# Rotary embedding in fp32 on one core: one GpSimd product over eight positions, paired PSUM banks, and the last stores on the other queue

## The chip, the cores and the metric

The kernel runs on one core of a Trainium2 chip. The metric is the device time of one execution in microseconds (us); the median of several executions counts, and lower is better.

## What is computed

```python
def reference(x, cos, sin):           # x: (8, 2048, 8, 64), cos and sin: (2048, 32), all float32
    x1 = x[..., : x.shape[-1] // 2]
    x2 = x[..., x.shape[-1] // 2 :]
    cos = cos[None, :, None, :]
    sin = sin[None, :, None, :]
    out1 = x1 * cos - x2 * sin
    out2 = x1 * sin + x2 * cos
    return np.concatenate([out1, out2], axis=-1)
```

Every head of 64 values is two halves of 32. Each output element is one element times a cosine, plus the element of the other half times a sine, whose sign is negative in the first half. The tables depend on the position in the sequence alone, so all eight heads and all eight batches share them.

## The kernel before, in words

**Layout.** The 2048 positions of a batch lie on 128 partitions, 16 consecutive positions on each. A position holds 8 heads of 64 values, so 512 floats; a batch is 8192 floats per partition, 4 MB in all. The tables are 16 x 32 floats per partition. The work goes by units of four positions (2048 floats per partition); batch 0 begins and batch 7 ends with two units of two positions.

**Loads and stores.** `xpool` has five tiles of a whole batch. Loads (line 67) are issued by SyncE (SP in the profile), that of batch 0 in three pieces with the tables between them. The first five batches are loaded ahead; the load of batch b + 5 (line 189) uses the tile of batch b and so waits until the stores of batch b have landed. The result is written over the input in the same tile. Stores (line 74) are issued by ScalarE (ACT): three pieces for batch 0, one for each of batches 1 to 6, three for batch 7. The text calls S6 or "store 6" the store of batch 6.

**One unit** (`rotate`, line 101) is made in one of three ways.
- Kind A, most units: GpSimd (POOL) makes two sine products into a tile `t2` in SBUF (line 121): the second output half from the first input half by `sin_sb`, and the first from the second by `nsin`, the negated table. VectorE (DVE) makes the cosine product into `t1` in PSUM (line 128), and adds the two into the batch's tile (line 135).
- Kind B, the first unit of batches 2, 4 and 5: the same products, with `t1` in SBUF, but TensorE (PE) adds them. For each 512 floats, two matmuls by the identity `eye` go into one PSUM bank `o`, the first for `t1` and the second for `t2` (lines 140 and 141), and ScalarE copies the bank into the batch's tile (line 142).
- Kind C, the first unit of batches 1 and 3: VectorE makes both products (lines 128 and 145), and TensorE adds them with `eye` and its negative `neye` (lines 156 and 157), ScalarE copies (line 161). GpSimd does nothing.

**What sets the order.** `keep` fixes the order of the instructions of each engine as they are written: unit by unit, batch by batch. So a store waits in ScalarE's stream until its batch is done, ahead of the copies of the next batch; the add of a unit stands on VectorE ahead of the next unit's cosine product. Semaphores are placed by the framework. A tile of a pool is given out again once all that reads or writes it is done. `t2` has three buffers of one unit each, `t1` in PSUM one (four banks), `t1s` in SBUF two, `o` two banks. The tables `cos_ps` and `sin_ps` hold two banks more[...].

**The beginning.** GpSimd makes `eye`; ScalarE makes `nsin`, `sin_ps` and `neye` (lines 89 to 91); VectorE copies the cosines to PSUM (line 92).

Of the kernel before, what the change touches and what calls it, by code (L numbers as in the profile page):

```python
# [9 lines left out]
@with_exitstack  # L10
def kernel(
    ctx: ExitStack,
    tc: tile.TileContext,
    x: bass.AP,
    cos: bass.AP,
    sin: bass.AP,
    out: bass.AP,
):
    nc = tc.nc
    keep = tc.keep_in_program_order  # L20
    f32 = mybir.dt.float32
    PSUM = bass.MemoryType.PSUM

    B, S, H, D = x.shape
    Dh = D // 2
    P = 128
    HD = H * D
    R = S // P
    ROW = R * HD
    UNIT = 4 * HD  # L30
    NBUF = 5
    C = 512
    last = B - 1

    xv = x.rearrange("b (q r) h d -> b q (r h d)", q=P)
    ov = out.rearrange("b (q r) h d -> b q (r h d)", q=P)
    cos_src = cos.rearrange("(q r) d -> q r d", q=P)
    sin_src = sin.rearrange("(q r) d -> q r d", q=P)

    const_pool = ctx.enter_context(tc.tile_pool(name="const", bufs=1))  # L40
    tab_pool = ctx.enter_context(tc.tile_pool(name="tab", bufs=1, space=PSUM))
    t1_pool = ctx.enter_context(tc.tile_pool(name="t1p", bufs=1, space=PSUM))
    o_pool = ctx.enter_context(tc.tile_pool(name="op", bufs=2, space=PSUM))
    t1s_pool = ctx.enter_context(tc.tile_pool(name="t1s", bufs=2))
    xpool = ctx.enter_context(tc.tile_pool(name="xpool", bufs=NBUF))
    t2_pool = ctx.enter_context(tc.tile_pool(name="t2p", bufs=3))

    cos_sb = const_pool.tile([P, R, Dh], f32, tag="cb")
    sin_sb = const_pool.tile([P, R, Dh], f32, tag="sb")
    nsin = const_pool.tile([P, R, Dh], f32, tag="ns")  # L50
    eye = const_pool.tile([P, P], f32, tag="eye")
    neye = const_pool.tile([P, P], f32, tag="neye")
    cos_ps = tab_pool.tile([P, R, Dh], f32, tag="cp")
    sin_ps = tab_pool.tile([P, R, Dh], f32, tag="sp")

    xts = {}

    def spans(sizes):
        lo = 0
        for n in sizes:  # L60
            yield lo, n
            lo += n

    def load(b):
        xt = xpool.tile([P, ROW], f32, tag="xt", name=f"xt{b}")
        for lo, n in spans([UNIT, UNIT, 2 * UNIT] if b == 0 else [ROW]):
            keep(nc.sync.dma_start(out=xt[:, lo : lo + n], in_=xv[b, :, lo : lo + n]))  # L67
            if b == 0 and lo == 0:
                keep(nc.sync.dma_start(out=cos_sb, in_=cos_src))  # L69
                keep(nc.sync.dma_start(out=sin_sb, in_=sin_src))  # L70
        xts[b] = xt

    def store(b, lo, n):
        keep(nc.scalar.dma_start(out=ov[b, :, lo : lo + n], in_=xts[b][:, lo : lo + n]))  # L74

    for b in range(NBUF):
        load(b)

    nc.gpsimd.memset(eye, 0.0)  # L79
    nc.gpsimd.affine_select(  # L80
        out=eye,
        in_=eye,
        compare_op=mybir.AluOpType.not_equal,
        fill=1.0,
        base=0,
        pattern=[[-1, P]],
        channel_multiplier=1,
    )
    keep(nc.scalar.mul(nsin, sin_sb, -1.0))  # L89
    keep(nc.scalar.copy(sin_ps, sin_sb))  # L90
    keep(nc.scalar.mul(neye, eye, -1.0))
    keep(nc.vector.tensor_copy(cos_ps, cos_sb))  # L92

    def rep(a, n):
        return dataclasses.replace(a, ap=[a.ap[0][:], a.ap[1][:], [0, n], a.ap[-1][:]])

    kinds = {}
    for b, kind in ((1, "C"), (2, "B"), (3, "C"), (4, "B"), (5, "B")):
        kinds[(b, 0)] = kind

    def rotate(b, lo, n):
        kind = kinds.get((b, lo), "A")
        xt = xts[b][:, lo : lo + n]
        r0 = lo // HD
        nr = n // HD
        xk = xt.rearrange("p (r k d) -> p r k d", r=nr, d=Dh)
        xu = xt.rearrange("p (g u d) -> p g u d", u=2, d=Dh)
        if kind == "A":
            t1 = t1_pool.tile([P, n], f32, tag="t1")
        else:  # L110
            t1 = t1s_pool.tile([P, n], f32, tag="t1s")
        if kind == "C":
            t2 = t1s_pool.tile([P, n], f32, tag="t1s")
        else:
            t2 = t2_pool.tile([P, n], f32, tag="t2")
        t1u = t1.rearrange("p (g u d) -> p g u d", u=2, d=Dh)
        t2u = t2.rearrange("p (g u d) -> p g u d", u=2, d=Dh)
        if kind != "C":
            for u, tab in ((1, sin_sb), (0, nsin)):
                keep(  # L120
                    nc.gpsimd.tensor_mul(  # L121
                        out=t2u[:, :, u, :].rearrange("p (r h) d -> p r h d", h=H),
                        in0=xu[:, :, 1 - u, :].rearrange("p (r h) d -> p r h d", h=H),
                        in1=rep(tab[:, r0 : r0 + nr, :], H),
                    )
                )
        keep(
            nc.vector.tensor_mul(  # L128
                out=t1.rearrange("p (r k d) -> p r k d", r=nr, d=Dh),
                in0=xk,  # L130
                in1=rep(cos_ps[:, r0 : r0 + nr, :], 2 * H),
            )
        )
        if kind == "A":
            keep(nc.vector.tensor_add(out=xt, in0=t1, in1=t2))  # L135
        elif kind == "B":
            for j in range(n // C):
                o = o_pool.tile([P, C], f32, tag="o")
                cs = slice(j * C, (j + 1) * C)
                nc.tensor.matmul(o, eye, t1[:, cs], start=True, stop=False)  # L140
                nc.tensor.matmul(o, eye, t2[:, cs], start=False, stop=True)  # L141
                keep(nc.scalar.copy(xt[:, cs], o))  # L142
        else:
            keep(
                nc.vector.tensor_mul(  # L145
                    out=t2.rearrange("p (r k d) -> p r k d", r=nr, d=Dh),
                    in0=xk,
                    in1=rep(sin_ps[:, r0 : r0 + nr, :], 2 * H),
                )
            )  # L150
            G = C // Dh
            for u in range(2):
                for j in range(n // 2 // C):
                    o = o_pool.tile([P, C], f32, tag="o")
                    gs = slice(j * G, (j + 1) * G)
                    nc.tensor.matmul(o, eye, t1u[:, gs, u, :], start=True, stop=False)  # L156
                    nc.tensor.matmul(  # L157
                        o, eye if u else neye, t2u[:, gs, 1 - u, :], start=False, stop=True
                    )
                    keep(  # L160
                        nc.scalar.copy(  # L161
                            xu[:, gs, u, :], o.rearrange("p (g d) -> p g d", d=Dh)
                        )
                    )

    def pieces(b):
        if b == 0:
            return [2 * HD, 2 * HD, UNIT, UNIT, UNIT]
        if b == last:
            return [UNIT, UNIT, UNIT, 2 * HD, 2 * HD]  # L170
        return [UNIT] * 4

    def shares(b):
        if b == 0:
            return [HD, 7 * HD, 2 * UNIT]
        if b == last:
            return [2 * UNIT, UNIT, UNIT]
        return [ROW]

    for b in range(B):  # L180
        done = 0
        outs = list(spans(shares(b)))
        for lo, n in spans(pieces(b)):
            rotate(b, lo, n)
            done = lo + n
            while outs and sum(outs[0]) <= done:
                store(b, *outs.pop(0))
        if b + NBUF <= last:
            load(b + NBUF)
# [30 lines left out]
```

## Time and profile before

| what | value |
|---|---|
| median of 8 executions | 163.46 us (163.33 to 164.02) |
| the profiled execution | 163.58 us |
| its span, first to last instruction | 161.7 us |
| VectorE busy | 140.1 us (87%), 66 instructions |
| GpSimd busy | 139.0 us (86%), 70 instructions |
| TensorE busy (matmuls) | 46.8 us (29%) |
| ScalarE busy | 14.3 us (9%) |
| moved by DMA | 67.65 MB, 418 GB/s over the span |

In the profile's slices the span is cut into 40 equal parts, and a digit is the busy share of a part in tenths, 9 meaning 90% or more. A queue line gives packets, MB, and the time that its packets took as a share of 16 DMA engines. A line of the chain of waits is start, duration, and what the time was spent on. A group line is line, engine and operation, output and inputs, shapes and count; then busy us and mean ns of one; then the idle time just before, and what ended most of it. A timeline line is start, duration, engine and line, with idle time before and its releaser in brackets. The fp32 matmuls stand in the trace as two records each (the "x2" of the timeline), 80 records for 40 matmuls.

### The profile page before, as it was taken

How to read it: one execution, taken by the hardware profiler on the slowest of the kernel's cores; microseconds unless marked ns; L12 is line 12 of the kernel's file. 1: busy time of each engine (PE TensorE's matmuls, PEld its weight loads, DVE VectorE, ACT ScalarE, POOL GpSimd, SP SyncE). 2: the span in 40 equal slices, each digit the busy share in tenths (PEclk: the TensorE clock that was granted, in tenths of full speed). 3: DMA queues.
4: the chain of work that ended last, by engine and by line, in shares of the span. 5: the costliest groups of instructions: out<-in, count | busy, mean ns of one | idle time of the engine just before them, and what ended most of it. 6: DMA issues, size and time to landing. Idle time of an engine off the chain costs nothing.

```text
span 161.7 us, 467 instructions
## 1 busy us (share of the span) xinstructions
PE 46.8 (29%) x80; PEld 18.6 (12%) x80; DVE 140.1 (87%) x66; ACT 14.3 (9%) x24; POOL 139.0 (86%) x70
## 2 busy tenths in 40 slices
PE   0000000399108940895029902990000000000000
PEld 0000000134003410331014301430000000000000
DVE  0458899999999999999999999999899998999900
ACT  3200000012100220022001310121000000000000
POOL 1299999999999899998996999998999979999200
PEclk9999999999855998579556995599655555555555
DMA  5999999899999999999999999999999999999994
GB/s 190 411 436 492 439 397 403 376 427 485 413 393 438 446 478 389 438 470 389 454 454 389 462 448 389 454 446 397 454 440 397 470 430 397 478 421 405 421 415 201
DMA packets 3458, 67.65 MB, mean 418 GB/s; under 512 B 384, under 2 KB 384, under 8 KB 768
## 3 DMA queue, kind: packets, MB, share of 16 engines
q1 hardware_dynamic: 1728, 34.08, 49.8%
q10 hardware_dynamic: 1728, 33.56, 48.2%
q14 instruction: 2, 0.02, 0.0%
HBM read 34.08 MB, written 33.55 MB: 418 GB/s over the span
## 4 chain that ended last, share of the span: by engine, by line
DMA 46%; DVE 37%; POOL 9%; issue 2%; SPq 1%; DVEq 0%; POOLq 0%; ACTq 0%
DMA xt<-in_x_dram 24%; DMA out_dram<-xt 19%; DVE t L128 18%; DVE xt L135 17%; POOL t L121 9%; DMA sin_sb<-in_sin_dram 3%; DVE t L145 1%; SPq L69 0%; SPq L67 0%; DVEq L135 0%; POOLq L121 0%; ACTq L74 0%
## 5 line engine op out<-in xcount | busy, mean ns | idle before, releaser
L121 POOL TENSOR_TENSOR t<-xt,sin_sb 128x1024 f32<-128x1024 f32 (+1 forms) x32 | 70.4, 2201 | 10.8 <-DMA sin_sb<-in_sin_dram 5.9
L128 DVE TENSOR_TENSOR t<-xt,cos_ps 128x2048 f32<-128x2048 f32 (+1 forms) x34 | 73.4, 2167 | 0.8
L121 POOL TENSOR_TENSOR t<-xt,nsin 128x1024 f32<-128x1024 f32 (+1 forms) x32 | 70.5, 2202 | 0.0
L135 DVE TENSOR_TENSOR xt<-t,t 128x2048 f32<-128x2048 f32 (+1 forms) x29 | 62.2, 2144 | 6.3 <-POOL t L121 3.8
L140 PE MATMUL o<-t,eye 128*128 128x512 f32 x24 | 16.0, 755 | 24.6 <-DVE t L128 24.6
L156 PE MATMUL o<-t,eye 128*128 128x512 f32 x16 | 11.7, 838 | 37.9 <-DVE t L128 37.9
L141 PE MATMUL o<-t,eye 128*128 128x512 f32 x24 | 14.9, 708 | 0.0
L142 ACT COPY xt<-o 128x512 f32<-128x512 f32 x12 | 7.0, 585 | 44.8 <-PE o L141 44.8
L140 PEld LDWEIGHTS o<-t,eye 128*128 128x128 f32 x24 | 5.7, 251 | 32.9 <-issue 32.9
L156 PEld LDWEIGHTS o<-t,eye 128*128 128x128 f32 x16 | 3.8, 257 | 42.8 <-POOL t L121 30.8
L161 ACT COPY xt<-o 128x512 f32<-128x512 f32 x8 | 4.7, 586 | 45.1 <-DVE t L128 26.6
L141 PEld LDWEIGHTS o<-t,eye 128*128 128x128 f32 x24 | 5.4, 227 | 7.8 <-issue 7.8
L92 DVE COPY cos_ps<-cos_sb 128x512 f32<-128x512 f32 x1 | 0.7, 695 | 6.2 <-DMA cos_sb<-in_cos_dram 6.2
L157 PE MATMUL o<-t,neye 128*128 128x512 f32 x8 | 5.6, 818 | 0.2 <-DVE t L145 0.2
L145 DVE TENSOR_TENSOR t<-xt,sin_ps 128x2048 f32<-128x2048 f32 x2 | 4.6, 2280 | 0.0
L157 PE MATMUL o<-t,eye 128*128 128x512 f32 x8 | 4.1, 592 | 0.0
L157 PEld LDWEIGHTS o<-t,neye 128*128 128x128 f32 x8 | 2.2, 294 | 4.5 <-issue 4.5
L157 PEld LDWEIGHTS o<-t,eye 128*128 128x128 f32 x8 | 1.5, 190 | 1.9 <-issue 1.9
L89 ACT ACT_TABLE_LOAD x1 | 1.3, 1283 | 0.7 <-PEq L204 0.7
L89 ACT ACTIVATE nsin<-sin_sb 128x512 f32<-128x512 f32 x1 | 0.6, 630 | 5.1 <-DMA sin_sb<-in_sin_dram 5.1
L90 ACT COPY sin_ps<-sin_sb 128x512 f32<-128x512 f32 x1 | 0.6, 579 | 0.0
L79 POOL MEMSET eye<- 128x128 f32 x1 | 0.2, 204 | 0.3 <-POOLq L204 0.3
(6 smaller groups left out, 1.0 us busy)
## 6 DMA issues: line engine op xcount, KB each, us to landing
xt<-in_x_dram SPq DMA_DIRECT2D x7, 4096.0 KB, 38.1
out_dram<-xt ACTq DMA_DIRECT2D x6, 4096.0 KB, 28.7
out_dram<-xt ACTq DMA_DIRECT2D x2, 2048.0 KB, 19.3
xt<-in_x_dram SPq DMA_DIRECT2D x2, 1024.0 KB, 6.1
xt<-in_x_dram SPq DMA_DIRECT2D x1, 2048.0 KB, 11.7
out_dram<-xt ACTq DMA_DIRECT2D x2, 1024.0 KB, 8.8
out_dram<-xt ACTq DMA_DIRECT2D x1, 1792.0 KB, 21.1
cos_sb<-in_cos_dram SPq DMA_DIRECT2D x1, 256.0 KB, 5.0
```

Source lines behind the costliest of these rows:

```text
L89: keep(nc.scalar.mul(nsin, sin_sb, -1.0))
L92: keep(nc.vector.tensor_copy(cos_ps, cos_sb))
L121: nc.gpsimd.tensor_mul(out=t2u[:, :, u, :].rearrange("p (r h) d -> p r h d", h=H), in0=xu[:, :, 1 - u, :].rearrange("p (r h) d -> p r h d" ...
L128: nc.vector.tensor_mul(out=t1.rearrange("p (r k d) -> p r k d", r=nr, d=Dh), in0=xk, in1=rep(cos_ps[:, r0 : r0 + nr, :], 2 * H),)
L135: keep(nc.vector.tensor_add(out=xt, in0=t1, in1=t2))
L140: nc.tensor.matmul(o, eye, t1[:, cs], start=True, stop=False)
L141: nc.tensor.matmul(o, eye, t2[:, cs], start=False, stop=True)
L142: keep(nc.scalar.copy(xt[:, cs], o))
L145: nc.vector.tensor_mul(out=t2.rearrange("p (r k d) -> p r k d", r=nr, d=Dh), in0=xk, in1=rep(sin_ps[:, r0 : r0 + nr, :], 2 * H),)
L156: nc.tensor.matmul(o, eye, t1u[:, gs, u, :], start=True, stop=False)
L157: nc.tensor.matmul(o, eye if u else neye, t2u[:, gs, 1 - u, :], start=False, stop=True)
L161: nc.scalar.copy(xu[:, gs, u, :], o.rearrange("p (g d) -> p g d", d=Dh))
```

## The change

Sync's queue issues the stores of the last batch. A unit of TensorE's sum is now four matmuls into two PSUM banks and one ScalarE copy of 1024 floats, with one such pair of banks. A sine product is one GpSimd instruction over eight positions (two of two and one of four at the beginning, two of four at the end): its input reads the two halves of each head in reversed order, by a negative step, and its table `sgn` holds minus sine and sine side by side, made by ScalarE in four passes. VectorE takes a product in parts of four positions. `t2` has two buffers of eight positions, `t1s` one, which first holds the tables as loaded. Kind C, `sin_ps` and `neye` are gone; the first unit of batches 1 to 5 is added on TensorE. The last batch's final positions go by units of four, not two of two.

```diff
--- before.py
+++ after.py
@@ -27,9 +27,9 @@
     HD = H * D
     R = S // P
     ROW = R * HD
-    UNIT = 4 * HD
     NBUF = 5
     C = 512
+    T = 4
     last = B - 1
 
     xv = x.rearrange("b (q r) h d -> b q (r h d)", q=P)
@@ -40,20 +40,22 @@
     const_pool = ctx.enter_context(tc.tile_pool(name="const", bufs=1))
     tab_pool = ctx.enter_context(tc.tile_pool(name="tab", bufs=1, space=PSUM))
     t1_pool = ctx.enter_context(tc.tile_pool(name="t1p", bufs=1, space=PSUM))
-    o_pool = ctx.enter_context(tc.tile_pool(name="op", bufs=2, space=PSUM))
-    t1s_pool = ctx.enter_context(tc.tile_pool(name="t1s", bufs=2))
+    o_pool = ctx.enter_context(tc.tile_pool(name="op", bufs=1, space=PSUM))
+    t1s_pool = ctx.enter_context(tc.tile_pool(name="t1s", bufs=1))
     xpool = ctx.enter_context(tc.tile_pool(name="xpool", bufs=NBUF))
-    t2_pool = ctx.enter_context(tc.tile_pool(name="t2p", bufs=3))
+    t2_pool = ctx.enter_context(tc.tile_pool(name="t2p", bufs=2))
 
-    cos_sb = const_pool.tile([P, R, Dh], f32, tag="cb")
-    sin_sb = const_pool.tile([P, R, Dh], f32, tag="sb")
-    nsin = const_pool.tile([P, R, Dh], f32, tag="ns")
+    tabs = t1s_pool.tile([P, 2, R, Dh], f32, tag="t1s", name="tabs")
+    cos_sb = tabs[:, 0, :, :]
+    sin_sb = tabs[:, 1, :, :]
+    sgn = const_pool.tile([P, R, 2, Dh], f32, tag="sg")
     eye = const_pool.tile([P, P], f32, tag="eye")
-    neye = const_pool.tile([P, P], f32, tag="neye")
     cos_ps = tab_pool.tile([P, R, Dh], f32, tag="cp")
-    sin_ps = tab_pool.tile([P, R, Dh], f32, tag="sp")
 
-    xts = {}
+    loads = {0: [4, 4, 8]}
+    products = {0: [2, 2, 4, 8], last: [8, 4, 4]}
+    stores = {0: [1, 7, 8], last: [8, 4, 4]}
+    on_tensor = {(b, 0) for b in range(1, 6)}
 
     def spans(sizes):
         lo = 0
@@ -61,17 +63,22 @@
             yield lo, n
             lo += n
 
+    xts = {}
+
     def load(b):
         xt = xpool.tile([P, ROW], f32, tag="xt", name=f"xt{b}")
-        for lo, n in spans([UNIT, UNIT, 2 * UNIT] if b == 0 else [ROW]):
-            keep(nc.sync.dma_start(out=xt[:, lo : lo + n], in_=xv[b, :, lo : lo + n]))
+        for lo, n in spans(loads.get(b, [R])):
+            cs = slice(lo * HD, (lo + n) * HD)
+            keep(nc.sync.dma_start(out=xt[:, cs], in_=xv[b, :, cs]))
             if b == 0 and lo == 0:
                 keep(nc.sync.dma_start(out=cos_sb, in_=cos_src))
                 keep(nc.sync.dma_start(out=sin_sb, in_=sin_src))
         xts[b] = xt
 
     def store(b, lo, n):
-        keep(nc.scalar.dma_start(out=ov[b, :, lo : lo + n], in_=xts[b][:, lo : lo + n]))
+        cs = slice(lo * HD, (lo + n) * HD)
+        queue = nc.sync if b == last else nc.scalar
+        keep(queue.dma_start(out=ov[b, :, cs], in_=xts[b][:, cs]))
 
     for b in range(NBUF):
         load(b)
@@ -86,104 +93,66 @@
         pattern=[[-1, P]],
         channel_multiplier=1,
     )
-    keep(nc.scalar.mul(nsin, sin_sb, -1.0))
-    keep(nc.scalar.copy(sin_ps, sin_sb))
-    keep(nc.scalar.mul(neye, eye, -1.0))
+    for lo, hi in ((0, 4), (4, R)):
+        keep(nc.scalar.mul(sgn[:, lo:hi, 0, :], sin_sb[:, lo:hi, :], -1.0))
+        keep(nc.scalar.copy(sgn[:, lo:hi, 1, :], sin_sb[:, lo:hi, :]))
     keep(nc.vector.tensor_copy(cos_ps, cos_sb))
 
-    def rep(a, n):
-        return dataclasses.replace(a, ap=[a.ap[0][:], a.ap[1][:], [0, n], a.ap[-1][:]])
+    def sine_product(b, lo, n):
+        xt = xts[b][:, lo * HD : (lo + n) * HD]
+        t2 = t2_pool.tile([P, n * HD], f32, tag="t2")
+        swapped = dataclasses.replace(
+            xt,
+            offset=xt.offset + Dh,
+            ap=[xt.ap[0][:], [HD, n], [D, H], [-Dh, 2], [1, Dh]],
+        )
+        s = sgn[:, lo : lo + n, :, :]
+        signed = dataclasses.replace(
+            s, ap=[s.ap[0][:], [D, n], [0, H], [Dh, 2], [1, Dh]]
+        )
+        keep(
+            nc.gpsimd.tensor_mul(
+                out=t2.rearrange("p (r h u d) -> p r h u d", r=n, h=H, u=2),
+                in0=swapped,
+                in1=signed,
+            )
+        )
+        return t2
 
-    kinds = {}
-    for b, kind in ((1, "C"), (2, "B"), (3, "C"), (4, "B"), (5, "B")):
-        kinds[(b, 0)] = kind
-
-    def rotate(b, lo, n):
-        kind = kinds.get((b, lo), "A")
-        xt = xts[b][:, lo : lo + n]
-        r0 = lo // HD
-        nr = n // HD
-        xk = xt.rearrange("p (r k d) -> p r k d", r=nr, d=Dh)
-        xu = xt.rearrange("p (g u d) -> p g u d", u=2, d=Dh)
-        if kind == "A":
-            t1 = t1_pool.tile([P, n], f32, tag="t1")
-        else:
-            t1 = t1s_pool.tile([P, n], f32, tag="t1s")
-        if kind == "C":
-            t2 = t1s_pool.tile([P, n], f32, tag="t1s")
-        else:
-            t2 = t2_pool.tile([P, n], f32, tag="t2")
-        t1u = t1.rearrange("p (g u d) -> p g u d", u=2, d=Dh)
-        t2u = t2.rearrange("p (g u d) -> p g u d", u=2, d=Dh)
-        if kind != "C":
-            for u, tab in ((1, sin_sb), (0, nsin)):
-                keep(
-                    nc.gpsimd.tensor_mul(
-                        out=t2u[:, :, u, :].rearrange("p (r h) d -> p r h d", h=H),
-                        in0=xu[:, :, 1 - u, :].rearrange("p (r h) d -> p r h d", h=H),
-                        in1=rep(tab[:, r0 : r0 + nr, :], H),
-                    )
-                )
+    def finish(b, lo, n, t2):
+        xt = xts[b][:, lo * HD : (lo + n) * HD]
+        pool, tag = (t1s_pool, "t1s") if (b, lo) in on_tensor else (t1_pool, "t1")
+        t1 = pool.tile([P, n * HD], f32, tag=tag)
+        c = cos_ps[:, lo : lo + n, :]
+        cosines = dataclasses.replace(
+            c, ap=[c.ap[0][:], c.ap[1][:], [0, 2 * H], c.ap[-1][:]]
+        )
         keep(
             nc.vector.tensor_mul(
-                out=t1.rearrange("p (r k d) -> p r k d", r=nr, d=Dh),
-                in0=xk,
-                in1=rep(cos_ps[:, r0 : r0 + nr, :], 2 * H),
+                out=t1.rearrange("p (r k d) -> p r k d", r=n, d=Dh),
+                in0=xt.rearrange("p (r k d) -> p r k d", r=n, d=Dh),
+                in1=cosines,
             )
         )
-        if kind == "A":
+        if (b, lo) not in on_tensor:
             keep(nc.vector.tensor_add(out=xt, in0=t1, in1=t2))
-        elif kind == "B":
-            for j in range(n // C):
-                o = o_pool.tile([P, C], f32, tag="o")
-                cs = slice(j * C, (j + 1) * C)
-                nc.tensor.matmul(o, eye, t1[:, cs], start=True, stop=False)
-                nc.tensor.matmul(o, eye, t2[:, cs], start=False, stop=True)
-                keep(nc.scalar.copy(xt[:, cs], o))
-        else:
-            keep(
-                nc.vector.tensor_mul(
-                    out=t2.rearrange("p (r k d) -> p r k d", r=nr, d=Dh),
-                    in0=xk,
-                    in1=rep(sin_ps[:, r0 : r0 + nr, :], 2 * H),
-                )
-            )
-            G = C // Dh
-            for u in range(2):
-                for j in range(n // 2 // C):
-                    o = o_pool.tile([P, C], f32, tag="o")
-                    gs = slice(j * G, (j + 1) * G)
-                    nc.tensor.matmul(o, eye, t1u[:, gs, u, :], start=True, stop=False)
-                    nc.tensor.matmul(
-                        o, eye if u else neye, t2u[:, gs, 1 - u, :], start=False, stop=True
-                    )
-                    keep(
-                        nc.scalar.copy(
-                            xu[:, gs, u, :], o.rearrange("p (g d) -> p g d", d=Dh)
-                        )
-                    )
-
-    def pieces(b):
-        if b == 0:
-            return [2 * HD, 2 * HD, UNIT, UNIT, UNIT]
-        if b == last:
-            return [UNIT, UNIT, UNIT, 2 * HD, 2 * HD]
-        return [UNIT] * 4
-
-    def shares(b):
-        if b == 0:
-            return [HD, 7 * HD, 2 * UNIT]
-        if b == last:
-            return [2 * UNIT, UNIT, UNIT]
-        return [ROW]
+            return
+        for j in range(n * HD // (2 * C)):
+            o = o_pool.tile([P, 2 * C], f32, tag="o")
+            for k in range(2):
+                cs = slice((2 * j + k) * C, (2 * j + k + 1) * C)
+                oc = o[:, k * C : (k + 1) * C]
+                nc.tensor.matmul(oc, eye, t1[:, cs], start=True, stop=False)
+                nc.tensor.matmul(oc, eye, t2[:, cs], start=False, stop=True)
+            keep(nc.scalar.copy(xt[:, 2 * j * C : 2 * (j + 1) * C], o))
 
     for b in range(B):
-        done = 0
-        outs = list(spans(shares(b)))
-        for lo, n in spans(pieces(b)):
-            rotate(b, lo, n)
-            done = lo + n
-            while outs and sum(outs[0]) <= done:
+        outs = list(spans(stores.get(b, [R])))
+        for lo, n in spans(products.get(b, [8, 8])):
+            t2 = sine_product(b, lo, n)
+            for at, m in spans([min(T, n)] * (n // min(T, n))):
+                finish(b, lo + at, m, t2[:, at * HD : (at + m) * HD])
+            while outs and sum(outs[0]) <= lo + n:
                 store(b, *outs.pop(0))
         if b + NBUF <= last:
             load(b + NBUF)

```

## The prediction

> **What bounds the kernel now.** I read the page's slices and queue table first.
>
> ```profile
> DVE  0458899999999999999999999999899998999900
> POOL 1299999999999899998996999998999979999200
> DMA  5999999899999999999999999999999999999994
> q1 hardware_dynamic: 1728, 34.08, 49.8%
> q10 hardware_dynamic: 1728, 33.56, 48.2%
> ```
>
> The two queues (q1 loads, q10 stores) fill 98.0% of 16 DMA engines over 161.7 us: transfers bound the kernel, the 2% being its two ends. VectorE and GpSimd follow closely, so little slowing is free.
>
> The chain of waits says the same from store b2 on, then passes to the products of batch 7:
>
> ```profile
> 63.22 30.24 DMA out_dram<-xt
> ...
> 93.54 38.20 DMA xt<-in_x_dram
> ...
> 131.87 4.62 POOL t L121 x2
> ...
> 152.22 1.22 DVE xt L135
> ```
>
> To see the slack I set store issues beside landings (DMA issues by window). The stores of batches 0 to 6 go out at 28.5 (batch 0's last), 47.0, 63.2, 81.7, 97.9, 114.4 and 133.6, and land at 54.7, 74.2, 93.5, 113, 131.9, 141.5 and 151.1. Each is issued before its predecessor lands, so the store queue never runs dry. The last three go out at 143.6, 148.3 and 153.5; the final one lands at 160.9, 7.4 us later, because others are ahead of it. A 1 MB transfer with no x transfer ahead took 4.7 us (the first load), so the final store could go out at 156.2 and cost nothing. VectorE ends at 153.4: the cover is 2.8 us.
>
> Durations come from the groups by shape:
>
> ```profile
> L128 DVE TENSOR_TENSOR t<-xt,cos_ps 128x2048 f32<-128x2048 f32 x30 | 68.5, 2292 | 0.7
> L121 POOL TENSOR_TENSOR t<-xt,nsin 128x1024 f32<-128x1024 f32 x28 | 65.4, 2337 | 0.0
> L135 DVE TENSOR_TENSOR xt<-t,t 128x2048 f32<-128x2048 f32 x25 | 57.3, 2291 | 4.4 <-POOL t L121 2.3
> L142 ACT COPY xt<-o 128x512 f32<-128x512 f32 x12 | 7.0, 585 | 44.8 <-PE o L141 44.8
> L91 ACT ACTIVATE neye<-eye 128x128 f32<-128x128 f32 x1 | 0.3, 300 | 0.0
> ```
>
> The stretch that decides my forecast is batch 4 in the timeline:
>
> ```profile
> 83.92 2.04 PE L140 MATMUL o<-t,eye 128*128 128x512 f32 x2 [8.81 <-DVE t L128]
> 86.09 2.29 DVE L135 TENSOR_TENSOR xt<-t,t 128x2048 f32<-128x2048 f32 x1
> 88.46 2.35 POOL L121 TENSOR_TENSOR t<-xt,sin_sb 128x1024 f32<-128x1024 f32 x1 [1.47 <-DVE xt L135]
> 91.77 1.02 PE L141 MATMUL o<-t,eye 128*128 128x512 f32 x2
> ```
>
> GpSimd reads input and writes t2; why should it wait for VectorE's add? Because the add, ending at 88.38, frees a t2 buffer. TensorE still holds another until 92.79. So even with three buffers a sum on TensorE makes GpSimd wait for a buffer.
>
> **The Trainium skill.** "GPSIMD Engine Reference", 3.1, puts a two-input product at 2.6 cycles per element, a floor of its one read port, and 2048 elements at 4497 ns. The trace agrees: starts lie 2.285 us apart at 1024 elements and 1.21 at 512, so 0.135 us plus 1.075 us per position of 512, durations 0.05 us longer; that makes 4.49 us at 2048. "DMA: Bandwidth & Descriptors", "Issuing engines are not separate DMA queues", says that transfers run on the same 16 engines whoever issues them. The shares above fit: 49.8 and 48.2% of one set. "TensorE: Matmul & The Clock Gate", "What's actually happening", gives some 3.4 us of work before the full clock. In the trace each sum on TensorE starts so: matmuls start 1.84 and 1.71 us apart, then 0.86.
>
> **The change part by part.**
>
> *Signed table.* Four ScalarE passes replace three. GpSimd now needs the first two (128 elements, 0.30 us like neye, the second issued some 0.25 us after the first), where it read sin_sb directly. Sine lands at 7.06; GpSimd starts at 7.7 instead of 7.21. Cost 0.5 us.
>
> *Products.* Two of 1024 elements per 4 positions (4.57 us) become one of 4096 per 8: 0.135 + 8 × 1.075 = 8.74 us, against 9.14. No row shows this pattern with its reversed halves. Its runs are still 32 elements, and the skill's plain 2048 costs what these do, so I take the line. Bounds: 7.4 us (a price hidden in the old halves' strided writes) to 9.6 (+10%). The two units of kind C give their sine from VectorE to GpSimd, so GpSimd does 128 positions, not 120: 19 × 0.135 + 128 × 1.075 = 140.2 us, against 139.0 busy. VectorE sheds 2 × 2.28 and some starts, about 4.9 us, but only in batches 1, 3 and 7; TensorE still takes five sums, none in batches 6 and 7.
>
> *Granularity.* An add now waits for eight positions, not four.
>
> *PSUM pairs.* A 1024-wide copy from rows 128 at 300 and 512 at 585 ns: about 0.96 us. There is one o buffer, so TensorE pauses for the first copy: 1.3 us more with its hand-over. A sum held TensorE 9.14, 8.87 and 9.27 us (kind B, first start to last end); now 10.4. Bounds: 9.1, if the pause is hidden, to 11.5, if the clock also drops. What stands behind ScalarE's copies is only the next store.
>
> *Two t2 buffers of eight positions, not three of four.* This is the decisive part. Product (b,0) is held until TensorE's last matmul; product (b,8) has the other; (b+1,0) must wait. Laid out instruction by instruction:
> - Products of batch 0 end at 9.99, 12.27, 16.7 and 25.4 us. The first load of batch 1 had landed by then (no wait at 25.75 in the trace). P(1,0) ends at 34.2, P(1,8) at 42.9.
> - VectorE: a pair, cosine product and add, takes 4.72 us from start to start. After P(0,8): add to 27.8, pair to 32.5, cosine of (1,0) to 34.8: 9.4 us after the product. TensorE then holds until 34.8 + 0.1 + 10.4 = 45.3. P(2,0) starts at 45.4, a stall of 2.4 us.
> - After the stall VectorE is ahead by about 1.8 us, TensorE can do its first cosine matmul before the product ends, and P(3,0) does not stall; P(4,0) does. Two batches take 9.4 + 10.5 + 2 × 8.74 = 37.4 us (GpSimd alone: 35.0).
> - P(2,0), P(4,0), P(6,0) start at 45.4, 82.9 and 120.4; P(6,0) ends at 129.1. From there VectorE is the bound, with nothing on TensorE: one add of 2.36 and seven pairs of 4.72: 164.5 us, 11.1 later than now. Products of batch 7 end before their adds need them (the last at 159.6).
>
> *DMA.* The count, sizes and order are the same. Stores of batches 1 to 5 go out at about 50, 70, 87, 107 and 125, still before their predecessors land. Store 6 goes out at 145.8, four us after store 5 lands: the queues run dry.
>
> *The last stores on SP.* SP's last load goes out at 93.5, so they queue behind nothing. They would pass store 6 if it were still running; it has nearly drained by 154.9. I cost this at nothing; the work that covers it is VectorE's own last pairs, since the last store follows the last add. If the old backlog were there, two store queues would share the same engines: nothing either.
>
> *Sum.* Last add 164.5, issue 0.1, a 1 MB store with nothing before it 4.7, last landing to the span's end 0.8 (161.7 − 160.9): span 170.1. The profiled execution took 163.58 for its span of 161.7, 1.88 around it; it lay 0.12 above the median 163.46. 170.1 + 1.88 − 0.12 = **171.9 us**.
>
> **Rivals.**
> - *No buffer stall* (TensorE releases within 8.0 us of the cosine, or it starts warm). For: cosine products could come earlier. Against: 1.84 + 1.71 us is paid at each start. Then P(5,8) ends at 112.8, VectorE reaches the add of (6,0) at 122.3 and ends at 157.7: span 163.3, **165.1 us**. Still slower, by coarser products and an all-VectorE end.
> - *The reversed pattern is dearer.* In my layout P(6,0) ends at 76.4 + 6 products; at 9.6 us each that is 5.2 us later: **177.1 us**. For: four-level patterns are new here; against: address steps cost nothing visible now.
> - *The wide product is much cheaper*, ending not slower. The last store may go out at 156.2, so P(6,0) must end by 120.7: 76.4 + 6p ≤ 120.7, p ≤ 7.4 us. Beyond it the DMA queues bound again and the time is at best that of full queues, some 0.7 us under now: **162.8 us**. For: one contiguous write replaces two strided ones. Against: the floor above, equal for contiguous operands.
> - *The change does only what its first words say*, the other parts hiding behind full DMA queues: **163.4 us**. This needs 2.8 us of cover to hold against 11.1; against it is the buffer wait already in the trace.
>
> **How the numbers follow.** Buffer stall 0.56; no stall 0.20; dearer pattern 0.14; cheaper product 0.06; no effect 0.04. Holding TensorE for 9.1 instead of 10.4 takes three stalls × 1.3 = 3.9 off, to 168.0; full stalls in the other two batches add 4.8. The range is 164.8 to 177.1, from just under the no-stall case to the dear one. A measurement here can tell about 0.2%. Faster 0.06, same 0.04, slower 0.90.
>
> **What would show it.** Right: products of about 8.74 us; GpSimd idle about 2 us before P(2,0), P(4,0), P(6,0), freed by TensorE's last matmul; VectorE waiting for products in batches 1 to 5 and unbroken in 6 and 7; the last add near 164; DMA slices below 9 after 141; a last store that lands some 5 us after its issue. Wrong: DMA full to the end, or VectorE done by 156.

## The result

| | before | changed |
|---|---|---|
| median | 163.46 us | 195.51 us (194.36 to 196.09) |
| profiled execution, span | 163.58, 161.7 us | 194.85, 193.1 us |
| GpSimd busy | 139.0 us | 142.3 us |
| VectorE busy | 140.1 us | 135.4 us |
| moved by DMA | 67.65 MB | 67.64 MB |

The ratio is 1.195, 95% interval 1.193 to 1.196: slower by 32 us, where the prediction had 8.4 us and a range up to 177.1. Medians and ratios, here and below, are of executions within 1.5% of their kernel's fastest; longer ones, which the kernel before has too (168.51 us, once in 35), are left out, and where many were, their number is given. The busy times moved by 3 to 5 us; what has grown is the idle time between. The slices and the queue table of the changed kernel:

```profile
DVE  0398379969992993628955479645593299999990
POOL 1499999986999059991399922999419999992900
DMA  6999999999999999999999999991009900079995
q1 hardware_dynamic: 2160, 38.27, 47.4%
q10 hardware_dynamic: 1296, 29.36, 35.8%
```

The DMA line is full up to slice 26, counting from 0, and then has holes: the queues together fill 83.2% of 16 engines, against 98.0%. GpSimd and VectorE, whose lines were 8s and 9s almost throughout, now have dips up to slice 31, GpSimd's in an even rhythm. So look for a wait of GpSimd that comes back once a batch. GpSimd's own timeline has it:

```profile
45.18 17.69 POOL L114 TENSOR_TENSOR t<-xt,sgn 128x4096 f32<-128x4096 f32 x2 [2.24 <-PE o L146]
69.98 17.64 POOL L114 TENSOR_TENSOR t<-xt,sgn 128x4096 f32<-128x4096 f32 x2 [7.11 <-issue]
94.74 17.65 POOL L114 TENSOR_TENSOR t<-xt,sgn 128x4096 f32<-128x4096 f32 x2 [7.11 <-issue]
119.51 17.65 POOL L114 TENSOR_TENSOR t<-xt,sgn 128x4096 f32<-128x4096 f32 x2 [7.11 <-issue]
144.26 30.88 POOL L114 TENSOR_TENSOR t<-xt,sgn 128x4096 f32<-128x4096 f32 x4 [7.11 <-issue]
```

Each row is a run of products that follow each other; a new row begins with a wait. P(2,0) is the product of batch 2 that begins at position 0. It waits 2.24 us for TensorE, as forecast (2.4). P(3,0), P(4,0), P(5,0) and P(6,0) wait 7.11 us each, and for nothing that the profile names. Some lines of the full timeline around the first of these say what they wait for:

```profile
53.99 8.88 POOL L114 TENSOR_TENSOR t<-xt,sgn 128x4096 f32<-128x4096 f32 x1
61.51 1.02 PE L146 MATMUL o<-t,eye 128*128 128x512 f32 x2
62.91 2.29 DVE L138 TENSOR_TENSOR xt<-t,t 128x2048 f32<-128x2048 f32 x1 [3.85 <-POOL t L114]
65.23 2.30 DVE L131 TENSOR_TENSOR t<-xt,cos_ps 128x2048 f32<-128x2048 f32 x1
67.56 2.29 DVE L138 TENSOR_TENSOR xt<-t,t 128x2048 f32<-128x2048 f32 x1
69.98 17.64 POOL L114 TENSOR_TENSOR t<-xt,sgn 128x4096 f32<-128x4096 f32 x2 [7.11 <-issue]
```

P(2,8) ends at 62.87. TensorE's last matmul on P(2,0) had ended at 62.53, so the buffer of P(2,0) was free. Yet P(3,0) starts at 69.98, just after VectorE's second add from P(2,8) ends at 69.85. P(3,0) was given the buffer of P(2,8), the product that had only just been written. The addresses in the built program agree; with A and B for the two of `t2`:

```
P(1,0) A  P(1,8) B      P(2,0) A  P(2,8) B
P(3,0) B  P(3,8) A      P(4,0) A  P(4,8) B
P(5,0) B  P(5,8) A      P(6,0) A  P(6,8) B
P(7,0) A  P(7,8) B      P(7,12) A
```

Four times a product follows another in the same buffer: before P(3,0), P(4,0), P(5,0), P(6,0), which are the four waits. GpSimd can then not start until VectorE has done an add, a cosine product and an add (6.98 us from the end of the product), and meanwhile the other buffer lies idle.

### The profile page after: what moved, and what is told of

It reads as the page before. It is cut to its first block, busy times and chain, and to the rows that moved or that the text cites. A ratio compares the mean times of both kernels' runs of the same rounds, so it can differ in the third digit from the quotient of the medians.

```text
span 193.1 us, 409 instructions
## 1 busy us (share of the span) xinstructions
PE 50.4 (26%) x80; PEld 18.2 (9%) x80; DVE 135.4 (70%) x62; ACT 12.7 (7%) x15; POOL 142.3 (74%) x25
## 2 busy tenths in 40 slices
DMA packets 3457, 67.64 MB, mean 350 GB/s; under 512 B 384, under 2 KB 384, under 8 KB 768
## 5 line engine op out<-in xcount | busy, mean ns | idle before, releaser
L114 POOL TENSOR_TENSOR t<-xt,sgn 128x4096 f32<-128x4096 f32 (+2 forms) x19 | 141.6, 7479 | 40.7 <-issue 28.4
L145 PE MATMUL o<-t,eye 128*128 128x512 f32 x40 | 28.7, 809 | 74.4 <-DVE t L131 68.7
L146 PE MATMUL o<-t,eye 128*128 128x512 f32 x40 | 26.5, 750 | 13.9 <-POOL t L114 13.9
L147 ACT COPY xt<-o 128x1024 f32<-128x1024 f32 x10 | 10.1, 1012 | 121.5 <-PE o L146 121.5
L145 PEld LDWEIGHTS o<-t,eye 128*128 128x128 f32 x40 | 9.1, 253 | 89.9 <-issue 44.6
L146 PEld LDWEIGHTS o<-t,eye 128*128 128x128 f32 x40 | 9.1, 240 | 29.7 <-POOL t L114 20.0
L99 DVE COPY cos_ps<-tabs 128x512 f32<-128x512 f32 x1 | 0.7, 694 | 6.2 <-DMA tabs<-in_cos_dram 6.2
L97 ACT ACTIVATE sgn<-tabs 128x128 f32<-128x128 f32 (+1 forms) x2 | 0.8, 414 | 4.8 <-DMA tabs<-in_sin_dram 4.8
L98 ACT COPY sgn<-tabs 128x128 f32<-128x128 f32 (+1 forms) x2 | 0.8, 388 | 0.0
```

The lines of the kernel that those rows point to most:

```text
L97: keep(nc.scalar.mul(sgn[:, lo:hi, 0, :], sin_sb[:, lo:hi, :], -1.0))
L98: keep(nc.scalar.copy(sgn[:, lo:hi, 1, :], sin_sb[:, lo:hi, :]))
L114: nc.gpsimd.tensor_mul(out=t2.rearrange("p (r h u d) -> p r h u d", r=n, h=H, u=2), in0=swapped, in1=signed,)
L145: nc.tensor.matmul(oc, eye, t1[:, cs], start=True, stop=False)
L146: nc.tensor.matmul(oc, eye, t2[:, cs], start=False, stop=True)
L147: keep(nc.scalar.copy(xt[:, 2 * j * C : 2 * (j + 1) * C], o))
```

## The experiments

My theory: the order of the buffers makes the time, four waits of 7.1 us. Rivals: products of eight positions force GpSimd and VectorE into turns whatever the buffer; TensorE's long hold of a buffer is the cause; one of the small parts (the queue, the paired banks, the reversed pattern) costs far more than thought.

**Strict turns.** The changed kernel with its two buffers named, so that they alternate:

```diff
-    t2_pool = ctx.enter_context(tc.tile_pool(name="t2p", bufs=2))
+    t2_pool = ctx.enter_context(tc.tile_pool(name="t2p", bufs=1))
...
-        t2 = t2_pool.tile([P, n * HD], f32, tag="t2")
+        turn[0] ^= 1
+        t2 = t2_pool.tile([P, n * HD], f32, tag=f"t2{turn[0]}", name=f"t2_{b}_{lo}")
```

> The changed kernel, but the two t2 buffers are named and take strict turns, so that the first product of a batch never gets the buffer of the product just before it. Buffer-turn theory (four products wait 7.1 us each because they were given the buffer that VectorE is still emptying): those waits go, GpSimd waits for TensorE about 2.4 us before the first products of batches 2, 4 and 6 and the time is 171.9 us, as the layout in the prediction had it. Rival, coarse products: an add that must wait for eight positions puts GpSimd and VectorE in turns whatever the buffer: above 188 us. Rival, the held buffer: TensorE's sum is what blocks, so the waits only move to it: 180 us or more.

Measured 171.93 us (170.51 to 173.05), ratio to before 1.051 (1.046 to 1.057). Beside the names nothing else changed, and 23.6 us are gone. GpSimd's timeline:

```profile
45.95 17.68 POOL L116 TENSOR_TENSOR t<-xt,sgn 128x4096 f32<-128x4096 f32 x2 [3.06 <-PE o L148]
65.28 17.67 POOL L116 TENSOR_TENSOR t<-xt,sgn 128x4096 f32<-128x4096 f32 x2 [1.65 <-PE o L148]
83.91 17.68 POOL L116 TENSOR_TENSOR t<-xt,sgn 128x4096 f32<-128x4096 f32 x2 [0.96 <-PE o L148]
103.81 17.67 POOL L116 TENSOR_TENSOR t<-xt,sgn 128x4096 f32<-128x4096 f32 x2 [2.21 <-PE o L148]
121.73 30.93 POOL L116 TENSOR_TENSOR t<-xt,sgn 128x4096 f32<-128x4096 f32 x4 [0.25 <-PE o L148]
```

The waits now name TensorE's last matmul, 8.1 us in all (3.06 + 1.65 + 0.96 + 2.21 + 0.25) against 7.2 in my layout; they don't fall on every second batch as cleanly as I had them. Coarse products, or the hold of TensorE, as the whole cause were expected to keep it at 180 or above; both are out, though both still have a part in what is left.

**One repeat, and four.** The turns again, with one product or four given the buffer of the one before:

```diff
-        turn[0] ^= 1
+        turn[0] ^= (b, lo) != (3, 0)
```

> The two buffers in strict turns, as in e1_turns, but for one product: the first of batch 3 is given the buffer of the product just before it, and turns go on from there. Buffer-turn theory, laid out as in the prediction: that product waits about 7.1 us for VectorE's add instead of 1.7 for TensorE, later waits shift, and VectorE's last add comes 4.6 us later than with turns: 171.9 + 4.6 = 176.5 us. If the order of the buffers were not the cause, one change of it would do nothing: 171.9 us.

```diff
-        turn[0] ^= 1
+        turn[0] ^= (b, lo) not in {(3, 0), (4, 0), (5, 0), (6, 0)}
```

> The two named buffers again, now in the very order of the changed kernel: the first products of batches 3, 4, 5 and 6 are given the buffer of the product just before. Buffer-turn theory: the changed kernel's time, 195.5 us, within 1 us, though the buffers are named as in e1_turns. If naming the buffers had helped in another way than by their order, it stays near 171.9 us.

One repeat: 177.13 us (177.00 to 177.42), 5.2 more than with turns. Four: 196.02 us (195.87 to 196.11), 24.1 more than with turns and the changed kernel's time within 0.6 us, with the buffers named as in the first experiment. One repeat shows a 7.11 us wait before P(3,0) alone:

```profile
44.75 17.67 POOL L116 TENSOR_TENSOR t<-xt,sgn 128x4096 f32<-128x4096 f32 x2 [1.78 <-PE o L148]
69.53 17.64 POOL L116 TENSOR_TENSOR t<-xt,sgn 128x4096 f32<-128x4096 f32 x2 [7.11 <-issue]
87.97 17.68 POOL L116 TENSOR_TENSOR t<-xt,sgn 128x4096 f32<-128x4096 f32 x2 [0.80 <-PE o L148]
```

So the cause can be put in and taken out, and the time grows with its dose.

**No sum on TensorE.**

```diff
-    on_tensor = {(b, 0) for b in range(1, 6)}
+    on_tensor = set()
```

> The changed kernel with no sum on TensorE: VectorE adds every unit (the five first units of batches 1 to 5 too). Products keep their eight positions and two buffers. Buffer-turn theory: without TensorE's hold the buffers are freed in turn, nothing waits 7 us, and VectorE is the bound: from the product's end at 25.4 us one add and 29 pairs of 4.72 us, 164.7, then 5.6 to the end of the span and 1.8 around it: 172 us, 23 us less than the changed kernel although VectorE has 11.5 us more work. Rival, coarse products: the waits stay and VectorE's extra work adds to them: 200 us or more.

Measured 170.32 us (172 was expected), ratio 1.042 (1.040 to 1.045): with five more adds on VectorE (147.8 us busy against 135.4) the kernel is 25 us faster than the changed one. Here the program, though not told to, gives the buffers in turns, and GpSimd's waits in steady state are 0.5 us each:

```profile
69.99 8.84 POOL L114 TENSOR_TENSOR t<-xt,sgn 128x4096 f32<-128x4096 f32 x1 [0.54 <-DVE xt L138]
79.36 8.85 POOL L114 TENSOR_TENSOR t<-xt,sgn 128x4096 f32<-128x4096 f32 x1 [0.53 <-DVE xt L138]
```

**Products of four, the same bytes.** Every other part of the change stays.

```diff
-    t2_pool = ctx.enter_context(tc.tile_pool(name="t2p", bufs=2))
+    t2_pool = ctx.enter_context(tc.tile_pool(name="t2p", bufs=4))
...
-    products = {0: [2, 2, 4, 8], last: [8, 4, 4]}
+    products = {0: [2, 2, 4, 4, 4], last: [4, 4, 4, 4]}
...
-        for lo, n in spans(products.get(b, [8, 8])):
+        for lo, n in spans(products.get(b, [4, 4, 4, 4])):
```

> The changed kernel with products of four positions and four t2 buffers of four, so the same bytes. Buffer-turn theory: with three other buffers no product needs the one that VectorE empties last, and the DMA queues bound again: 163.4 us, within 1 us. Rival, the hold of TensorE by paired banks (10.5 us per sum, one pair): 168 us or more. Rival, the price of the reversed pattern: GpSimd's products would be above 4.7 us per four positions; expected 4.5 us.

Measured 163.61 us in 15 of 20 executions, ratio 1.0018 (1.0006 to 1.0029); the other five took 165.9 to 170.3. The slices:

```profile
POOL 1199999999999999999999999999999999999300
DMA  5999999899999999999999999999999999999995
```

GpSimd is unbroken and the DMA engines are full to the end, as before the change. GpSimd's products of four took 4.54 us on average, under the 4.7 that a price of the reversed pattern would have shown. The kernel is no faster: the work that the change saves is not what binds.

**The three small parts, each alone on the kernel before.** The queue:

```diff
-        keep(nc.scalar.dma_start(out=ov[b, :, lo : lo + n], in_=xts[b][:, lo : lo + n]))
+        queue = nc.sync if b == last else nc.scalar
+        keep(queue.dma_start(out=ov[b, :, lo : lo + n], in_=xts[b][:, lo : lo + n]))
```

> The kernel before with one edit: the last batch's three stores go out on sync's queue. Every theory that has the stores share 16 DMA engines: 163.4 us, within 0.3 us, since the store of batch 6 and the last three share the same engines; the last store can land no earlier than the backlog. Rival, two store queues fill the engines better than one: up to 0.5 us less. Rival, they disturb each other: up to 0.7 us more.

Paired banks, in kind B (kind C uses one bank of the pair):

```diff
-    o_pool = ctx.enter_context(tc.tile_pool(name="op", bufs=2, space=PSUM))
+    o_pool = ctx.enter_context(tc.tile_pool(name="op", bufs=1, space=PSUM))
...
-            for j in range(n // C):
-                o = o_pool.tile([P, C], f32, tag="o")
-                cs = slice(j * C, (j + 1) * C)
-                nc.tensor.matmul(o, eye, t1[:, cs], start=True, stop=False)
-                nc.tensor.matmul(o, eye, t2[:, cs], start=False, stop=True)
-                keep(nc.scalar.copy(xt[:, cs], o))
+            for j in range(n // (2 * C)):
+                o = o_pool.tile([P, 2 * C], f32, tag="o")
+                for k in range(2):
+                    cs = slice((2 * j + k) * C, (2 * j + k + 1) * C)
+                    oc = o[:, k * C : (k + 1) * C]
+                    nc.tensor.matmul(oc, eye, t1[:, cs], start=True, stop=False)
+                    nc.tensor.matmul(oc, eye, t2[:, cs], start=False, stop=True)
+                keep(nc.scalar.copy(xt[:, 2 * j * C : 2 * (j + 1) * C], o))
```

> The kernel before with kind B alone on paired banks: one o buffer of two banks, copies of 1024 (kind C keeps copies of 512, but has one buffer of o instead of two). The hold of a sum grows by 1.3 us in three batches, by 1.3 or more in the two of kind C; the DMA queues hide up to 2.8 us at the end. Expected 163.4 us, within 0.5. Rival, the longer hold reaches GpSimd through its third buffer and the cover is used up: 165 to 167 us.

The signed product, over four positions:

```diff
-            for u, tab in ((1, sin_sb), (0, nsin)):
-                keep(
-                    nc.gpsimd.tensor_mul(
...
+            keep(
+                nc.gpsimd.tensor_mul(
+                    out=t2.rearrange("p (r h u d) -> p r h u d", r=nr, h=H, u=2),
+                    in0=swapped,
+                    in1=signed,
+                )
+            )
```

> The kernel before with the signed-sine product alone: one product of 2048 elements per four positions in place of two of 1024 (kinds A and B), the table made by ScalarE in four passes, three t2 buffers as before; the loaded tables lie in a t1s buffer to make room. GpSimd takes about 4.5 us per four positions in place of 4.57, and its first add comes some 0.1 us later. The DMA queues bind: 163.4 us, within 0.4. Rival, the reversed pattern costs: 165 us or more.

Queue 163.37 us, ratio 0.9991 (0.9980 to 1.0001); pairs 163.59, 1.0011 (1.0000 to 1.0021); signed product 163.43 (10 of 12 executions), 1.0001 (0.9992 to 1.0011). By these intervals none differs from the kernel before by more than some 0.2%.

**What is left above 163 us.** Two trials on the turns. Single banks again:

```diff
-    o_pool = ctx.enter_context(tc.tile_pool(name="op", bufs=1, space=PSUM))
+    o_pool = ctx.enter_context(tc.tile_pool(name="op", bufs=2, space=PSUM))
...
+        for j in range(n * HD // C):
+            o = o_pool.tile([P, C], f32, tag="o")
+            cs = slice(j * C, (j + 1) * C)
+            nc.tensor.matmul(o, eye, t1[:, cs], start=True, stop=False)
+            nc.tensor.matmul(o, eye, t2[:, cs], start=False, stop=True)
+            keep(nc.scalar.copy(xt[:, cs], o))
```

> The two buffers in strict turns, as in e1_turns, and TensorE's sum back to single banks with one copy of 512 each (two buffers of o). The hold of a sum falls from 10.5 to about 9.1 us, so the three waits of some 2.4 us lose 1.3 each: 168.0 us. If the wait for TensorE no longer matters (VectorE alone sets the end), 171.9 us stays. If the pairing costs nothing, the same.

Measured 168.3 us, ratio 1.030 (1.028 to 1.032), from two of four executions (167.94 and 168.59; the others took 170.49 and 170.85). That is 3.7 less than with pairs, and 3.9 less was expected. The size is rough, since the four executions with turns and pairs spread over 2.5 us, but GpSimd's waits for TensorE agree: 3.6 us in all (1.87 + 0.41 + 1.29) against 8.1.

```profile
44.82 35.34 POOL L116 TENSOR_TENSOR t<-xt,sgn 128x4096 f32<-128x4096 f32 x4 [1.87 <-PE o L146]
80.57 17.69 POOL L116 TENSOR_TENSOR t<-xt,sgn 128x4096 f32<-128x4096 f32 x2 [0.41 <-PE o L146]
99.55 48.60 POOL L116 TENSOR_TENSOR t<-xt,sgn 128x4096 f32<-128x4096 f32 x6 [1.29 <-PE o L146]
```

So the longer hold of paired banks does cost here, where on the kernel before it was hidden. Then sums in batches 6 and 7 too:

```diff
-    on_tensor = {(b, 0) for b in range(1, 6)}
+    on_tensor = {(b, 0) for b in range(1, 8)}
```

> The turns and single banks of e7_single, and TensorE also adds the first units of batches 6 and 7. If what is left above the kernel before is VectorE's unbroken end (P(6,0) and then an add and seven pairs), two adds of 2.36 us leave it: 169.5 - 4.7 = 164.8 us, or some 166 if GpSimd's waits for TensorE take part of that back. If coarse products or the waits alone set it: 169.5 us stays.

Measured 169.01 us, ratio 1.033 (1.029 to 1.037), where some 165 to 166 was expected: a miss, and by more than it seems. The expectation started from 169.5, the median of all four executions with single banks; from 168.3 it would have been 163.6. Lines from the timeline's end:

```profile
152.89 1.02 PE L146 MATMUL o<-t,eye 128*128 128x512 f32 x2
154.00 4.50 POOL L116 TENSOR_TENSOR t<-xt,sgn 128x2048 f32<-128x2048 f32 x1 [4.34 <-PE o L146]
158.53 2.29 DVE L140 TENSOR_TENSOR xt<-t,t 128x2048 f32<-128x2048 f32 x1 [2.58 <-POOL t L116]
```

VectorE did get ahead, but the last product has to wait until TensorE has read P(7,0) out of its buffer, and VectorE then waits 2.58 us for the product. Much of the saved adds comes back as this wait. The last add still ends 1.2 us earlier than with single banks alone (160.82 against 162.00), but the last store then takes 5.0 us to land, not 3.8, and the profiled spans are 166.9 and 166.7.

Products of four in the same bytes had left almost nothing above the kernel before, so what is left with turns comes with products of eight in two buffers. How much of it is waiting for TensorE, and how much VectorE's unbroken end, was separated only in part. No version tried is faster than the kernel before beyond what can be told.

## Why the prediction was wrong

The direction was right, and so was the resource, the two `t2` buffers; the size was wrong by a factor of nearly four (32.05 us against 8.4), and one step made it so.

**The step that failed** is "product (b,0) is held until TensorE's last matmul; product (b,8) has the other; (b+1,0) must wait", with "P(3,0) does not stall". It took for granted that buffers are used in turns. P(2,0) was so (2.24 us measured, 2.4 forecast, start at 45.18 against 45.4). In batches 3 to 6 the program gave the first product the buffer just filled. A batch then takes 24.76 us on GpSimd from start to start (17.65 for two products, and the wait of 7.11) where I had 18.7; over four batches the difference is 24.2 us, and P(6,0) ended at 153.08 where I had 129.1. With turns forced, the same layout gave 171.9 and the chip 171.93. Part of that closeness is luck: the single waits differ, and the executions lie between 170.51 and 173.05.

**Terms that held**, from the changed kernel's profile:
- A product of eight positions: 8.85 us mean, 8.79 from start to start; forecast 8.74. The reversed pattern cost at most 0.05 us beyond the line through the smaller shapes, so the rival "dearer pattern" is out, and so is the cheaper product. The 4497 ns that the prediction took from the Trainium skill ("GPSIMD Engine Reference", 3.1) are for an add; the changed kernel's products of 2048 took 4511 ns on average.
- GpSimd's start 7.41, forecast 7.7: the table cost 0.2 us, not 0.5.
- ScalarE's wide copy 1.01 us (forecast 0.96); TensorE's hold in batch 1 from 34.63 to 45.10, 10.5 (forecast 10.4).
- From the end of P(6,0) VectorE runs unbroken to the end, as the chain of waits shows:

```profile
137.16 7.10 issue
144.26 8.82 POOL t L114
153.08 0.02 issue
153.10 2.30 DVE xt L138
...
186.07 2.29 DVE xt L138
```

The last add ends at 188.36, 35.3 us after P(6,0); forecast 35.4. The span ends 4.7 us later; forecast 5.6.
- The stores moved to SP: nothing, as costed. This was tried on the kernel before alone (163.37 us), where the DMA engines are full.
- The Trainium skill's statement that transfers share the same 16 engines whichever engine issues them ("DMA: Bandwidth & Descriptors", "Issuing engines are not separate DMA queues") agrees with that run.

**DMA** ran dry only as a consequence: store 4 went out at 119.46 and landed 14.1 us later; store 5 went out at 144.21 and landed 11.1 us later, store 6 at 169.46. The holes in slices 27 to 34 are the gaps between.

**What the profile before already showed.** The wait that I quoted, a product starting 0.08 us after an add frees its buffer while TensorE holds another, was a product taking a buffer out of turn. It was P(4,12), and it got the buffer of P(4,4), not that of P(4,0), whose turn it would have been. There that choice did no harm. All three buffers were still in use when GpSimd became free, at 86.99; the one given came free first, at 88.38, TensorE's at 92.79, and the third only with the add of P(4,8), at 93.10:

```profile
90.81 2.29 DVE L135 TENSOR_TENSOR xt<-t,t 128x2048 f32<-128x2048 f32 x1
```

So "the buffers are short" was a right reading of this wait. What I did not ask is which buffer each product gets next, and the answer, not a rotation, was already there. In the changed kernel the buffer given came free last of the two, and the wait was 7.11 us.

Why the framework gave the buffers in that order was not looked into and stays open.

## What to carry to other kernels

Where a pool has few buffers with consumers of unequal length, find out which buffer each use gets before laying out a schedule; don't assume a rotation, and name buffers apart if the order matters. A wait of "issue" that ends right after another engine's instruction can be a dependency that the profile didn't name, as it was here: compare the start with the ends around it, and test the guess. And ask what binds before saving work: here VectorE shed 4.7 us of work while full DMA queues set the time, so that only the loss of overlap could show.

## What the runs showed of the hardware

GpSimd's fp32 product lay close to a line over the shapes tried: 1.21 and 2.285 us from start to start at 512 and 1024 elements in the kernel before, 8.79 at 4096 in the changed one, whose input is read in reversed halves, by a negative step (the line through the two smaller shapes gives 8.74). Two store queues did no better than one for the last 8 MB (163.37 against 163.41 us in the same comparison).
